# A Hymba-style layer on one core: products 7 and 4 on one-bank accumulators, the late work of two feed-forward tiles spread over 16 steps, four sums moved to GpSimd

## The chip, the core and the metric

The kernel runs on one core of one Trainium2 chip. A core has TensorE (PE in the profile; its weight loads are PEld), VectorE (DVE), ScalarE (ACT), GpSimd (POOL) and SyncE (SP), each with a queue of its own that is worked off in order; they wait for one another through semaphores. SP issues nearly all DMAs. PE writes into PSUM, eight banks of 512 f32 for each of 128 partitions; everything else of the core lives in SBUF. The metric is the device time of one execution in microseconds (us); lower is better.

## The reference

One inference step of a hybrid decoder layer for 1040 prompt tokens (16 meta tokens and 1024 others) and 8 sample tokens, 1048 tokens in all, with width 1024 and a feed-forward width of 2816:

```
h = h + 0.5 * swiglu(rmsnorm(h, n1), w1g, w1u, w1d)      # feed-forward 1
u = rmsnorm(h, nm) @ w_in                                # HGRN2 heads and Mamba-2 heads
h = h + concat(hgrn_out, ssm_out) @ w_out
h = h + 0.5 * swiglu(rmsnorm(h, n2), w2g, w2u, w2d)      # feed-forward 2
def swiglu(x, wg, wu, wd):
    return (jax.nn.silu(x @ wg) * (x @ wu)) @ wd
```

and a final RMSNorm of what remains. All is f32. The change touches the two feed-forward blocks alone: `x @ wg`, `x @ wu`, the product with SiLU, and the preparation of the operands of `@ wd`.

## The kernel before, in words

**Precision.** Every f32 operand is split into a high part and a rest (`hi`: a cast on ACT; `lo`: a subtraction on DVE), and every product is three matmuls: high by high, high by low, low by high (`mm3`, lines 163 to 165). One matmul has 262 columns in the first feed-forward block (Q = 1048/4) and 258 in the second, which works on the 1032 tokens that are left.

**Seven products.** `x @ [wg wu]` is cut into 2 by 2 blocks and computed in Strassen-Winograd form, with products that the code numbers 1 to 7. `Left` (line 468) makes the weights' operands of a 128-column tile of gate and up: `load` brings four pieces (1, 7, 4, 2) by DMA into `r` buffers, `sum_` (line 487, DVE) makes 5, 6, 7 and 3 of them, `hi` (line 491, ACT) and `lo` (line 495, DVE) split each into a `ws` buffer. There are 8 `r` buffers, 6 `ws` buffers and 9 temporaries `t`. The tokens' operands (`Blocks`) are made once and stay.

**Steps.** `Steps` is an order of work written out by hand. `add` appends a step: one product on one half of the tokens (c = 0 or 1), 4 x 3 = 12 matmuls, and what follows it (`post`: the evacuation of PSUM). `before(i, fn)` puts DVE, ACT or SP work ahead of step i; of several things ahead of one step, the one registered first goes first. PE, DVE, ACT and SP execute in the order in which `run` issues, and a queue whose head waits holds all that is behind it. GpSimd is not on that list.

**Units.** Most of a feed-forward block is made of units of two tiles, f = 0 and f = 1 (`two_pairs`, line 860): 9 units in the first block, 10 in the second. Each tile has the six products `ORDER2` = 1, 6, 2, 5, 7, 4, each for both halves: 12 steps. The seventh product, 3, is made for both tiles together with half as many matmuls by a second application of the same algorithm (`Third`): seven small products of 6 matmuls each, which follow steps 3 to 9 of tile f = 1 and use the four one-bank accumulators of the pool `mis` (`psm`). So a unit is 24 x 12 + 7 x 6 = 330 matmuls. Ahead of the units stand one or two single tiles of seven full products (`pair`, line 555), and in the first block also two plain tiles; behind the units stands the down projection (`down`).

**Accumulators.** The pool `acc` has the other four banks, as two buffers of two banks, one bank for each half. Products 1, 6, 5 and 7 begin an accumulator; 2 goes on top of 1, and 4 on top of 7, after the first of each has been read out: what is added is the sum so far.

```
        b = {2: 1, 3: 5, 4: 7}.get(p, p)
            new = p in (1, 6, 5, 7)
```

**What follows the products** (`post`, lines 894 to 908): 1 is copied by ACT (line 896); 6 (line 898), 5 (line 902), 7 (line 904, each half by itself) and 4 (line 907, both halves together) are added by DVE; 2 is multiplied by the norm's factor on DVE (line 885) and goes through SiLU on ACT (line 886). After 4, `out` (lines 889 and 892) scales up and multiplies it with the gate into the unit's hidden tile (`s` buffers, 8 of them). The gate and up parts that need `Third` follow at steps 10 to 13 of tile 1 and a little beyond it (`second`, `out`).

**Operands of the down projection.** `Hidden` takes the four hidden blocks of a unit, makes four differences (`sub`, line 965, DVE) and stores seven blocks to DRAM (`store`, line 968, SP), where `down` reads them later (line 1003). `jobs_apart` places the sums and stores of a unit at steps that mostly lie in the next unit, and earlier in the last unit.

Of the kernel before, what the change touches and what calls it, by code (L numbers as in the profile page):

```python
# [17 lines left out]
P = 128  # L18
# [49 lines left out]
class Core:  # L68
# [21 lines left out]
    def banks(self, n):  # L90

        self.banks_.close()
        self.acc = self.banks_.enter_context(self.tc.tile_pool(name="acc", bufs=4 // n, space=PSUM))
        self.pairs = n == 2

# [374 lines left out]
class Left:  # L470
# [30 lines left out]
    def plan(self, S, s0, late, sums, order=ORDER, loads=(-11, -11, -10, -10)):  # L501
        for ps, ds, fn in (
            ((7, 4, 1, 2) if len(order) == 6 else (1, 7, 4, 2), loads, self.load),
            ((5, 6, 7, 3), [d + sums for d in (-7, -7, -6, -5)], self.sum_),
            (order, [2 * i - 4 + late for i in range(7)], self.hi),
            (order, [2 * i - 3 + late for i in range(7)], self.lo),
        ):
            for p, d in zip(ps, ds):
                S.before(s0 + d, lambda p=p, fn=fn: fn(p))
# [9 lines left out]
class Unit:  # L519


    def __init__(self, K, w, ops, n, post, apart=()):
        self.K, self.w, self.ops, self.n, self.post, self.apart = K, w, ops, n, post, apart
        self.ps = {}
# [12 lines left out]
    def step(self, S, p, c, cs, mis=False):  # L537
# [5 lines left out]
        if p in self.apart:  # L543
            S.add(mm, lambda: self.post(p, slice(c, c + 1), self.bank(p, cs, mis)[:, c : c + 1]))
        else:
            S.add(mm, (lambda: self.post(p, slice(cs[0], cs[-1] + 1), self.bank(p, cs, mis))) if c == cs[-1] else None)
# [164 lines left out]
ORDER2 = (1, 6, 2, 5, 7, 4)  # L711
# [64 lines left out]
class Third:  # L776
# [7 lines left out]
    def plan(self, S, s1):  # L784
        for d, fn, *args in (
            (-2, self.sums, 0),
            (-1, self.sums, 1),
            (0, self.hi, 0),
            (1, self.lo, 0),
            (1, self.hi, 1),  # L790
            (2, self.lo, 1),
            (2, self.sums, 2),
            (3, self.hi, 2),
            (4, self.lo, 2),
            (5, self.hi, 3),
            (6, self.lo, 3),
        ):
            S.before(s1 + d, lambda fn=fn, args=args: fn(*args))
# [61 lines left out]
def two_pairs(K, S, wg, wu, i, ops, spread, hids, sub):  # L860
# [6 lines left out]
    cs = slice(0, 2)  # L867
# [9 lines left out]
    third.plan(S, s1)  # L877
# [6 lines left out]
    def gate(f, n, t, src):  # L884
        nc.vector.tensor_mul(t, src, spread.lanes(n, cs))  # L885
        nc.scalar.activation(t, t, AF.Silu)  # L886

    def out(f, n, u):
        nc.vector.tensor_mul(u, u, spread.lanes(n, cs))  # L889
        if not hids[f]:  # L890
            hids[f].append(K.slot("s", K.T))
        nc.vector.tensor_mul(halves(hids[f][0][:, n * 2 * K.Q : n * 2 * K.Q + 2 * K.Q]), temp(f, f"g{n}"), u)  # L892

    def post(f, p, c, b):
        if p == 1:
            nc.scalar.copy(temp(f, "v"), b)
        elif p == 6:
            nc.vector.tensor_add(temp(f, "v"), b, temp(f, "v"))
        elif p == 2:
            gate(f, 0, temp(f, "g0"), b)  # L900
        elif p == 5:
            nc.vector.tensor_add(temp(f, "g1"), b, temp(f, "v"))  # L902
        elif p == 7:
            nc.vector.tensor_add(temp(f, "u1")[:, c], b, temp(f, "g1")[:, c])  # L904
        elif p == 4:
            u = temp(f, "v")
            nc.vector.tensor_add(u, b, u)
            out(f, 0, u)

    def second(f):  # L910
        g = temp(f, "g1")
        nc.vector.tensor_add(g, g, third.q[f])  # L912
# [1623 lines left out]
```

## Time and profile before

| | us |
|---|---|
| median of three runs | 2018.33 (2015.95 to 2020.79) |
| profiled execution | 2022.06 |
| span of the profiled execution | 2019.8 |
| PE busy in the span | 1937.9 (96%) |
| DVE busy | 1537.6 (76%) |
| ACT busy | 859.2 (43%) |
| POOL busy | 84.7 (4%) |

The span runs from the first instruction to the last; the profiled execution's own time is 2.3 us longer than its span. A line such as L904 is a line of the kernel. `acc<-u,ws` says that an instruction writes the tile `acc` and reads `u` and `ws`, buffer numbers left out. "Idle before, releaser" is the time that an engine stood still ahead of an instruction, and what it had waited for. A matmul of 258 columns is shown with about 285 ns from its start to its end, but matmuls are pipelined, and starts follow one another much closer than that: the time that PE loses is read from the distances of starts, not from the busy time. In the timeline the first column is the start, the second the duration, and the bracket the idle time and its releaser.

The stretches: the units of the first feed-forward block lie at about 122 to 518 us, its down projection after that to about 750 us, the heads up to about 1230 us, the output projection up to about 1300 us, the units of the second block at about 1340 to 1780 us.

### The profile page before, as it was taken

How to read it: one execution, taken by the hardware profiler on the slowest of the kernel's cores; microseconds unless marked ns; L12 is line 12 of the kernel's file. 1: busy time of each engine (PE TensorE's matmuls, PEld its weight loads, DVE VectorE, ACT ScalarE, POOL GpSimd, SP SyncE). 2: the span in 40 equal slices, each digit the busy share in tenths (PEclk: the TensorE clock that was granted, in tenths of full speed). 3: DMA queues.
4: the chain of work that ended last, by engine and by line, in shares of the span. 5: the costliest groups of instructions: out<-in, count | busy, mean ns of one | idle time of the engine just before them, and what ended most of it. 6: DMA issues, size and time to landing. Idle time of an engine off the chain costs nothing.

```text
span 2019.8 us, 41324 instructions
## 1 busy us (share of the span) xinstructions
PE 1937.9 (96%) x16686; PEld 1886.4 (93%) x16686; DVE 1537.6 (76%) x2787; ACT 859.2 (43%) x1642; POOL 84.7 (4%) x144
## 2 busy tenths in 40 slices
PE   9989999999999999999999999989999999999998
PEld 9979999899999999999899989989999989999998
DVE  7878788888789778576575556987778888878974
ACT  6522222323543654466564446632222332353353
POOL 3000000000000320000000002200000000000000
PEclk9999999999999999999999999999999999999999
DMA  7132223223787651231453343222323332488762
GB/s 236 51 114 85 90 85 107 90 82 124 228 262 245 190 179 39 54 105 46 118 167 91 96 148 128 85 84 88 97 84 90 102 93 82 126 228 254 262 188 94
DMA packets 324209, 258.46 MB, mean 128 GB/s; under 512 B 18923, under 2 KB 298731, under 8 KB 324011
## 3 DMA queue, kind: packets, MB, share of 16 engines
q1 hardware_dynamic: 323779, 255.79, 41.3%
q8 instruction: 131, 2.15, 0.4%
q14 instruction: 59, 0.48, 0.1%
q0 software_dynamic: 224, 0.04, 0.0%
q10 hardware_dynamic: 16, 0.00, 0.0%
HBM read 190.79 MB, written 65.05 MB: 127 GB/s over the span
## 4 chain that ended last, share of the span: by engine, by line
PE 74%; DVE 20%; issue 3%; ACT 2%; DMA 1%; POOL 0%; SPq 0%; DVEq 0%; ACTq 0%; POOLq 0%
PE acc L163 21%; PE acc L165 20%; PE acc L164 20%; DVE r L487 3%; DVE ws L495 2%; DVE s L965 2%; DVE s L892 2%; DVE t L885 2%; PE mis L163 2%; PE mis L165 2%; PE mis L164 2%; DVE t L889 1%; DVE t L912 1%; DVE t L904 1%; DVE t L902 1%
## 5 line engine op out<-in xcount | busy, mean ns | idle before, releaser
L163 PE MATMUL acc<-u,ws 128*128 128x258 f32 (+4 forms) x4210 | 1241.4, 295 | 54.4 <-DVE t L904 40.7
L165 PE MATMUL acc<-u,ws 128*128 128x258 f32 (+4 forms) x4210 | 1223.4, 291 | 9.7 <-DVE ws L495 9.7
L164 PE MATMUL acc<-u,ws 128*128 128x258 f32 (+4 forms) x4210 | 1221.2, 290 | 1.1 <-DVE u L376 0.8
L163 PEld LDWEIGHTS acc<-u,ws 128*128 128x128 f32 x4210 | 797.0, 189 | 77.2 <-DVE t L904 32.2
L165 PEld LDWEIGHTS acc<-u,ws 128*128 128x128 f32 x4210 | 797.3, 189 | 15.2 <-DVE ws L495 14.7
L164 PEld LDWEIGHTS acc<-u,ws 128*128 128x128 f32 x4210 | 799.7, 190 | 2.4 <-DVE u L376 1.1
L495 DVE TENSOR_TENSOR ws<-r,ws 128x512 fp32r<-128x512 f32 x264 | 182.4, 692 | 15.7 <-ACT ws L491 15.5
L886 ACT ACTIVATE t<-t 128x516 f32<-128x516 f32 (+1 forms) x76 | 48.6, 640 | 338.0 <-DVE t L885 338.0
L491 ACT CAST ws<-r 128x512 fp32r<-128x512 f32 x264 | 152.9, 616 | 4.8 <-DVE r L487 4.7
L487 DVE TENSOR_TENSOR r<-r,r 128x512 f32<-128x512 f32 x149 | 102.9, 692 | 5.1 <-DMA r<-in_w_ffn_up_dram 3.7
L1011 DVE TENSOR_TENSOR u<-u,u 128x1048 fp32r<-128x1048 f32 (+3 forms) x84 | 97.9, 1166 | 8.6 <-ACT u L1007 8.2
L158 DVE TENSOR_TENSOR ws<-r,ws 128x512 fp32r<-128x512 f32 x88 | 60.9, 701 | 38.7 <-ACT ws L157 38.3
L250 POOL TENSOR_TENSOR t<-t,t 128x262 f32<-128x262 f32 (+1 forms) x56 | 54.5, 985 | 828.3 <-DMA r<-in_w_ffn_down_dram 641.7
L820 ACT CAST ws<-t 128x512 fp32r<-128x512 f32 (+1 forms) x57 | 31.2, 547 | 133.3 <-DVE t L809 85.6
L1069 ACT CAST ws<-u 128x512 fp32r<-128x512 f32 (+1 forms) x72 | 42.2, 585 | 100.4 <-DVE u L1064 92.6
L1007 ACT CAST u<-u 128x1048 fp32r<-128x1048 f32 (+3 forms) x84 | 82.9, 987 | 4.2 <-DMA u<-hd 4.2
L1069 ACT CAST ws<-r 128x512 fp32r<-128x512 f32 (+1 forms) x84 | 48.0, 582 | 71.0 <-DVE r L1064 28.5
L1098 DVE SCALAR_TENSOR_TENSOR s<-acc,s 128x524 f32<-128x524 f32 (+3 forms) x86 | 53.9, 650 | 31.7 <-PE acc L165 31.4
L1074 DVE TENSOR_TENSOR ws<-r,ws 128x512 fp32r<-128x512 f32 (+1 forms) x84 | 57.0, 687 | 25.0 <-ACT ws L1069 24.9
L163 PE MATMUL mis<-u,ws 128*128 128x258 f32 (+1 forms) x228 | 65.0, 285 | 2.2 <-DVE t L852 2.0
L904 DVE TENSOR_TENSOR t<-acc,t 128x258 f32<-128x258 f32 (+1 forms) x76 | 32.6, 428 | 43.8 <-PE acc L165 41.9
L1074 DVE TENSOR_TENSOR ws<-u,ws 128x512 fp32r<-128x512 f32 (+1 forms) x72 | 47.4, 659 | 23.7 <-ACT ws L1069 23.7
(459 smaller groups left out, 2416.8 us busy)
## 6 DMA issues: line engine op xcount, KB each, us to landing
r<-in_w_ffn_down_dram SPq DMA_DIRECT2D x128, 256.0 KB
hd<-s SPq DMA_DIRECT2D x93, 258.0 KB
r<-in_w_ffn_gate_dram SPq DMA_DIRECT2D x88, 256.0 KB
r<-in_w_ffn_up_dram SPq DMA_DIRECT2D x88, 256.0 KB
hd<-s SPq DMA_DIRECT2D x77, 262.0 KB
u<-hd SPq DMA_DIRECT2D x36, 516.0 KB
u<-hd SPq DMA_DIRECT2D x28, 524.0 KB
r<-in_w_in_dram SPq DMA_DIRECT2D x56, 256.0 KB
```

What stands on the lines that cost most here:

```text
L158: self.nc.vector.tensor_sub(lo, src, hi.bitcast(F32))
L163: mm(ps, whi, xhi, start=first, stop=False, skip_group_check=more)
L164: mm(ps, whi, xlo, start=False, stop=False, skip_group_check=more)
L165: mm(ps, wlo, xhi, start=False, stop=last, skip_group_check=more)
L250: K.nc.gpsimd.tensor_add(self.sq[q], self.sq[q], t)
L487: self.K.nc.vector.tensor_tensor(self.raw[p], self.raw[x], self.raw[y], op)
L491: self.K.nc.scalar.copy(self.w[p][:, : self.n * P], self.raw[p])
L495: self.K.nc.vector.tensor_sub(t[:, 512 : 512 + w], self.raw[p], t[:, :w].bitcast(F32))
L1007: K.nc.scalar.copy(hi, lo.bitcast(F32))
L1011: K.nc.vector.tensor_sub(lo, lo.bitcast(F32), hi.bitcast(F32))
L1069: nc.scalar.copy(w[p, j, g][:, : n * P], src)
L1074: nc.vector.tensor_sub(t[:, 512 : 512 + n * P], box[0], t[:, : n * P].bitcast(F32))
```

## The change

- **Accumulators.** The pool `acc` gets two fixed buffers of two banks each, `acc0` and `acc1`. In the units, products 1 and 2 use `acc0`, and 6 and then 5 use `acc1`. Everywhere else (`pair`, `down`) the two are taken in strict turn. Products 7 and 4 of the units go to the one-bank accumulators of `mis`, a bank for each half, beside the four that `Third` takes.
- **Order of the products.** A tile's order is 1, then product 4 of the tile before, then 6, 2, 5, 7. Product 4 of the last tile of a unit comes in the next unit, and of the last unit just ahead of `down`. With d counted from a unit's beginning: 0 and 1 are product 1 of f = 0; 2, 3 product 4 of the tile before; 4, 5 product 6; 6, 7 product 2; 8, 9 product 5; 10, 11 product 7; 12, 13 product 1 of f = 1; 14, 15 product 4 of f = 0; 16 to 23 products 6, 2, 5, 7 of f = 1. `Third`'s seven products follow the steps 14 to 20. The first unit has no product 4 ahead of it and is two steps shorter.
- **Read-out of 4.** DVE adds each half of product 4 by itself.
- **Late work.** What was in `second` and `out` stands at d = 16 to 31. A unit's last 8 of these positions lie in the next unit.
- **Weights.** `plan_apart` loads pieces 7, 4, 1, 2 at 10, 9, 9, 7 steps ahead of a tile, sums 5, 6, 7, 3 at 5, 4, 3, 2 ahead, and splits each operand about four steps ahead of its product.
- **Down's operands.** The four differences of a unit run on GpSimd instead of DVE, and stores and differences have new positions, the same in the last unit. One load of the first product of `down` is a step later.

```diff
-        self.acc = ...tile_pool(name="acc", bufs=4 // n, space=PSUM))
+        self.acc = ...tile_pool(name="acc", bufs=4 if n == 1 else 1, space=PSUM))
+        self.turn = 0
...
-    def psum2(self):
+    def psum2(self, i=None):
         assert self.pairs
-        return self.acc.tile([P, 2, 512], F32, tag="acc", name=self.uid("acc"))
+        if i is None:
+            i, self.turn = self.turn, 1 - self.turn
+        else:
+            self.turn = 1 - i
+        return self.acc.tile([P, 2, 512], F32, tag=f"acc{i}", name=self.uid("acc"))
...
+    def plan_apart(self, S, s0):
+        for fn, at in (
+            (self.load, ((7, -10), (4, -9), (1, -9), (2, -7))),
+            (self.sum_, ((5, -5), (6, -4), (7, -3), (3, -2))),
+            (self.hi, ((1, -4), (6, 0), (2, 2), (5, 4), (7, 6), (4, 10))),
+            (self.lo, ((1, -3), (6, 1), (2, 3), (5, 5), (7, 7), (4, 11))),
+        ):
+            for p, d in at:
+                S.before(s0 + d, lambda p=p, fn=fn: fn(p))
...
 class Third:
-    def plan(self, S, s1):
...
+    def plan(self, S, s0):
+        for fn, at in (
+            (self.sums, (10, 11, 14)),
+            (self.hi, (11, 12, 14, 16)),
+            (self.lo, (12, 13, 15, 17)),
+        ):
...
-def two_pairs(K, S, wg, wu, i, ops, spread, hids, sub):
+def two_pairs(K, S, wg, wu, i, ops, spread, hids, sub, before):
-    s0 = len(S.steps)
-    s1 = s0 + 2 * len(ORDER2)
+    s0 = len(S.steps) - (0 if before else 2)
...
-        lefts[n].plan(S, (s0, s1)[n], 0, 0, ORDER2, (-11, -10, -10, -9))
+        lefts[n].plan_apart(S, s0 + 12 * n)
...
+    def bank(f, p, c):
+        d = banks[f]
+        if p in (7, 4):
+            if c not in d:
+                d[c] = K.psm()[:, : K.Q]
+            return d[c]
+        n = {1: "a", 2: "a", 6: "b", 5: "c"}[p]
+        if n not in d:
+            d[n] = K.psum2(0 if n == "a" else 1)[:, :, : K.Q]
+        return d[n] if c is None else d[n][:, c]
...
         elif p == 4:
-            u = temp(f, "v")
-            nc.vector.tensor_add(u, b, u)
-            out(f, 0, u)
+            nc.vector.tensor_add(temp(f, "v")[:, c], bank(f, p, c), temp(f, "v")[:, c])
...
     for f in range(2):
+        steps(f, 1)
+        if f == 0 and before:
+            before()
+        elif f == 1:
+            steps(0, 4)
+        for p in (6, 2, 5, 7):
+            steps(f, p)
...
+    for d, fn, *args in (
+        (16, lambda: times_r(0, temp(0, "v"))),
+        (16, out, 0, 0),
+        (22, g1, 0),
+        (23, lambda: (times_r(1, temp(0, "g1")), silu(temp(0, "g1")))),
+        (24, lambda: times_r(1, temp(0, "u1"))),
+        (25, out, 0, 1),
+        (26, g1, 1),
+        (28, lambda: (times_r(1, temp(1, "g1")), silu(temp(1, "g1")))),
+        (28, lambda: times_r(0, temp(1, "v"))),
+        (29, out, 1, 0),
+        (30, lambda: times_r(1, temp(1, "u1"))),
+        (31, out, 1, 1),
+    ):
+        S.before(s0 + d, lambda fn=fn, args=args: fn(*args))
+    return s0, lambda: steps(1, 4)
...
-    def parts(self, i, hid):
+    def parts(self, i, hid, apart=False):
+        engine = K.nc.gpsimd if apart else K.nc.vector
...
-            K.nc.vector.tensor_sub(b[p], val(x), val(y))
+            engine.tensor_sub(b[p], val(x), val(y))
...
-    def jobs_apart(self, S, i, hid, s1):
...
+    def jobs_apart(self, S, i, hid, s0):
+        sub, store = self.parts(i, hid, True)
+        for d, args in zip((26, 32, 33, 34), ((5, 12, 1), (6, 3, 5), (7, 3, 12), (4, 2, 6))):
+            S.before(s0 + d, lambda args=args: sub(*args))
+        for d, p in zip((17, 29, 32, 33, 35, 36, 38), (1, 5, 3, 2, 6, 7, 4)):
+            S.before(s0 + d, lambda p=p: store(p))
```

More of the change, by code (lines that the diff above doesn't have):

```diff
@@ L915, in third_step @@
-    def third_step(m):
-        third.mm(m)
-        third.post(m)
-    for f in range(2):
-        unit = Unit(K, lefts[f].w, [o.op for o in ops], 4, lambda p, c, b, f=f: post(f, p, c, b), (7,))
-        for p in ORDER2:
-            for c in range(2):
-                j = len(S.steps) - s1
-                unit.step(S, p, c, (0, 1))
-                if 3 <= j < 10:
-                    S.also(lambda m=SUB[j - 3]: third_step(m))
-    S.before(s1 + 10, lambda: second(0))
-    S.before(s1 + 11, lambda: out(0, 1, temp(0, "u1")))
@@ L929, in two_pairs, with steps, mm @@
-    S.before(s1 + 12, lambda: second(1))
-    S.before(s1 + 13, lambda: out(1, 1, temp(1, "u1")))
-    return s1
+            nc.vector.tensor_add(temp(f, "v")[:, c], bank(f, p, c), temp(f, "v")[:, c])
+    def steps(f, p):
+        for c in range(2):
+            def mm(c=c):
+                new = p in (1, 6, 5, 7)
+                product(K, bank(f, p, c), lefts[f].w[p], ops[c].op[p], 4, new, True, not new)
+            S.add(mm, (lambda c=c: post(f, p, c)) if c == 1 or p in (7, 4) else None)
+            j = len(S.steps) - 1 - s0 - 14
+            if 0 <= j < len(SUB):
+                S.also(lambda j=j: (third.mm(SUB[j]), third.post(SUB[j])))
```

85 lines of the change are left out of this document (31 added, 54 removed).

## The prediction

> **What bounds the kernel now.** First the page's busy shares and the chain that ended last, then PE's waits.
>
> ```profile
> PE 1937.9 (96%) x16686; PEld 1886.4 (93%) x16686; DVE 1537.6 (76%) x2787; ACT 859.2 (43%) x1642; POOL 84.7 (4%) x144
> PEclk9999999999999999999999999999999999999999
> PE 74%; DVE 20%; issue 3%; ACT 2%; DMA 1%; POOL 0%; SPq 0%; DVEq 0%; ACTq 0%; POOLq 0%
> PE acc L163 <- DVE t L904: 40.7, 40, 3.4
> PE acc L165 <- DVE ws L495: 9.7, 23, 0.5
> ```
>
> PE runs at full clock and is the bound; a gain has to be time in which PE stands still. Its largest wait by far is for L904, the read-out of product 7: 40 times, about once for each of the 38 tiles. One unit of the first block in PE's timeline:
>
> ```profile
> 347.26 0.28 PE L165 MATMUL acc<-u,ws 128*128 128x262 f32 x1
> 347.68 0.39 PE L163 MATMUL acc<-u,ws 128*128 128x262 f32 x1
> 347.91 0.28 PE L164 MATMUL acc<-u,ws 128*128 128x262 f32 x1
> 348.65 0.39 PE L165 MATMUL acc<-u,ws 128*128 128x262 f32 x1 [0.46 <-DVE ws L495]
> 349.97 0.28 PE L163 MATMUL acc<-u,ws 128*128 128x262 f32 x1
> 355.69 0.28 PE L165 MATMUL acc<-u,ws 128*128 128x262 f32 x1
> 357.30 0.39 PE L163 MATMUL acc<-u,ws 128*128 128x262 f32 x1 [1.33 <-DVE t L904]
> 358.74 0.28 PE L165 MATMUL acc<-u,ws 128*128 128x262 f32 x1
> 359.64 0.36 PE L163 MATMUL acc<-u,ws 128*128 128x262 f32 x1 [0.61 <-DVE t L904]
> ```
>
> The 48 matmuls from 349.97 to 355.69 follow each other by 5.72/47 = 0.122 us; a step of 12 is 1.46 us. Counted in steps, the row at 347.68 is product 2's first half, 354.35 product 7's first half, 357.30 its second, 359.64 product 4. So the second half of 7 waits for the read-out of the *first* half, in another bank of the same tile, and 4 waits for that of the second. Lost beyond 0.12 a matmul: 0.30 + 0.11 + 0.62 = 1.03 us at product 2, and 1.49 + 0.78 = 2.27 us at 7 and 4; with the slow starts just after each jump (0.1 each) about 1.1 and 2.5: 3.6 us a unit. What DVE and ACT did:
>
> ```profile
> 345.98 0.64 ACT L886 ACTIVATE t<-t 128x524 f32<-128x524 f32 x1 [4.32 <-DVE t L885]
> 347.04 0.59 ACT L896 COPY t<-acc 128x524 f32<-128x524 f32 x1
> 356.01 0.70 DVE L902 TENSOR_TENSOR t<-acc,t 128x524 f32<-128x524 f32 x1
> 356.81 0.43 DVE L904 TENSOR_TENSOR t<-acc,t 128x262 f32<-128x262 f32 x1
> 359.06 0.43 DVE L904 TENSOR_TENSOR t<-acc,t 128x262 f32<-128x262 f32 x1 [1.22 <-PE acc L165]
> 347.68:391.61 43.93, 41.40 (x331) 40.51 (x331) 35.56 (x62) 12.60 (x25) 0.00 (x0) 1.00 0.30 92
> 1403.17:1446.64 43.47, 40.89 (x330) 40.03 (x330) 35.27 (x62) 12.52 (x24) 0.00 (x0) 1.00 0.30 92
> ```
>
> Product 1's copy (L896) waited behind the previous unit's last SiLU, which waited for DVE: the late work bunched at a unit's end. DVE reads 7's first half at 356.81 though the product had ended at about 355.7, being behind with L902. The last two rows are whole units of the two blocks: 43.93 and 43.47 us, against 330 x 0.122 = 40.2 of matmuls. DVE has 35.6 of them.
>
> **The change part by part.** *Stalls in the steady units.* With 7 and 4 a bank for each half, 7's second half waits for nothing; between 7 and 4 of a half lie one 7, two of product 1: three steps, 4.4 us, for a read-out that comes 1.5 to 2.5 us after its product in the rows above. Product 2 now has 4 and 6, four steps, behind product 1's copy (before: 6, two), and the last SiLU ahead of that copy is issued two steps before it. Product 5, in `acc1`, needs 6 read out, with product 2's two steps (2.9 us) between; 1 of the next tile needs 2 read out, four steps earlier. `mis` hands out eight banks a unit from four buffers: 7, 7, four of `Third`, 7, 7. The closest reuse is `Third`'s third bank at d = 17, when the bank of product 4's first half was read out at d = 14, or of the copy at d = 16, one step earlier: covered. The buffers `ws`, `r` and `t` have at most 7, 8 and 8 wanted at once against 6, 8 and 9; the seventh `ws` is `Third`'s last split at d = 16, held until `Third`'s second product has ended; it is wanted at d = 19, three steps on, and DVE's `lo` at d = 17 waits with it, ahead of 6's read-out, which is due a step later. As before, this hides in ACT and DVE time. So all 3.6 us a unit can go: 8 units of the first block with this pattern and 9 of the second, 17 x 3.6 = 61.2 us.
>
> *GpSimd.* Rows of POOL's only large use, and of DVE beside it:
>
> ```profile
> L965 DVE TENSOR_TENSOR s<-s,s 128x524 f32<-128x524 f32 x33 | 22.9, 697 | 0.0
> 389.79 0.70 DVE L965 TENSOR_TENSOR s<-s 128x524 f32<-128x524 f32 x1
> 390.41 0.70 DVE L889 TENSOR_TENSOR t<-t,u 128x524 f32<-128x524 f32 x1
> L2146 POOL TENSOR_TENSOR u<-u,u x3: 1273/1298/1298, 2003.3 to 2005.8; 128x512 f32<-128x512 f32 x2, 8x512 f32<-8x512 f32 x1
> 669.29 6.87 POOL L250 TENSOR_TENSOR t<-t,t 128x262 f32<-128x262 f32 x4 [6.83 <-ACT t L249]
> 673.75 1.80 DVE L1011 TENSOR_TENSOR u<-u,u 128x1048 fp32r<-128x1048 f32 x1
> 675.48 1.24 DVE L1074 TENSOR_TENSOR ws<-r,ws 128x512 fp32r<-128x512 f32 x1
> 677.25 1.24 DVE L1011 TENSOR_TENSOR u<-u,u 128x1048 fp32r<-128x1048 f32 x1
> ```
>
> Four L965 leave DVE, 0.62 us each from start to start (389.79 to 390.41): 2.5 us a unit. On POOL one takes about 1.33 (1298 ns x 524/512). It isn't free to DVE: beside POOL's 262-wide additions the same L1011 takes 1.80 instead of 1.24, and a 512-wide L1074 1.24, where the 524-wide rows above have 0.70: 0.55 us each. Estimated by width, a 524-wide one costs DVE at most 1.1 us; nothing where DVE reads PSUM or waits. Splitting 4's read-out adds 2 x (2 x 0.43 - 0.70) = 0.3. DVE's unit: 35.6 - 2.5 + 0.3 = 33.4, plus 0 to 4.4, so 33.4 to 37.8 against 40.2 of PE. It fits as a sum; the place to look at is d = 5 to 11. There DVE has, at 0.61 a full SBUF operation, 0.7 from PSUM and 0.4 a half: d=5 two and 6's read-out 1.9; d=6 0.6; d=7 three and 2's read-out 2.5; d=8 0.6; d=9 two and 5's 1.9; d=10 1.7; d=11 1.35: 10.6 us in 7 x 1.46 = 10.2, and three of the four GpSimd sums fall into it: up to 3.3 us late at its end. What is due then: product 1's weights at d = 12 (`lo` at d = 9), 4's at d = 14 (`lo` at d = 11), `Third`'s first at the end of d = 14. Counting through in that worst case, they come 0.2 to 0.3 us ahead of PE; from d = 14 a step with its `Third` product is 2.2 us and DVE catches up. So the residue runs from 0 to some 1.5 us a unit; I take 0.4, nearer to zero because the sum above is already the worst overlap: 17 x 0.4 = 7 back.
>
> The Trainium skill, "SBUF — State Buffer", section "SBUF: two separate sides", says that VectorE and GpSimd share a port pair that is locked for a whole instruction, also against a VectorE operation with two SBUF inputs, and that the other blocks fully. The rows agree in kind, with 0.55 us where POOL's own row is longer. Held for the whole 1.33 us it would be 5.3 us a unit and a DVE of 38.7; by that rule the residue would rise by about 0.6 a unit, and the sum end some 10 us higher.
>
> *Queues.*
>
> ```profile
> 125.51 0.56 SPq L481 DMA_DIRECT2D r<-in_w_ffn_up_dram  x1
> 131.80 0.69 DVE L487 TENSOR_TENSOR r<-r,r 128x512 f32<-128x512 f32 x1 [3.71 <-DMA r<-in_w_ffn_up_dram]
> ```
>
> SP issues per unit the same 8 loads and 7 stores. A store waits for its sum and holds the loads behind it. The closest: store 4 at d = 38 (14 of the next unit) stands ahead of loads 7, 4, 1 at 14 and 15. The last sum would end at about d = 34.5 if POOL starts after `out` at d = 31 and runs three times 1.33: two steps early or more. Loads have four steps to the first `sum_`, at least 5.9 us; in the worst case seen (the rows above, 125.51 to 131.80) it took 6.3. Cost 0 to 0.5 a unit, in the 0.4.
>
> *First units, ends and single tiles.*
>
> ```profile
> PE acc L163 <- DVE t L904: 2.5, 2, 1.9
> PE acc L163 <- DVE t L885: 2.0, 1, 2.0
> PE acc L163 <- DVE t L904: 4.0, 2, 3.4
> PE acc L163 <- DVE t L885: 1.2, 1, 1.2
> PE acc L163 <- DVE t L898: 0.8, 1, 0.8
> PE mis L163 <- DVE t L852: 1.0, 1, 1.0
> PE acc L163 <- DVE t L904: 0.4, 1, 0.4
> 1327.42 0.70 DVE L577 TENSOR_TENSOR t<-acc,u 128x516 f32<-128x516 f32 x1 [0.30 <-PE acc L165]
> 80.83 0.70 DVE L577 TENSOR_TENSOR t<-acc,u 128x524 f32<-128x524 f32 x1 [0.34 <-PE acc L165]
> ```
>
> PE's waits in 122 to 143 us (rows 1, 2), 1340 to 1365 (rows 3 to 5) and, the same at 500 to 520 and at 1765 to 1780, rows 6 and 7. First units: 4.5 and 6.0 us; there 5 follows the read-out of 2 (L885), and no longer will. DVE is behind by the `sub` blocks' making; I keep 0.5 and 2.5 of them: 7.5 saved (between 4 and 10.5). Last units: 1.4 each; product 4 now stands directly behind 7, while `down` already claims DVE: I put 2 each, +1 in all (-3 to +5). Single tiles (`pair`): the fixed turn puts product 5 into 2's buffer, so PE stands from 2's end until its read-out: 0.3 + 0.7 = 1.0 us by the last two rows. Three tiles; the middle one already runs behind DVE. +2 (0 to 4). The later load of `down` has five steps still: 0.
>
> Sum: -61 + 7 - 7.5 + 1 + 2 = -58.5, rounded to -60 for the start spacings left out above. The profiled execution, 2022.1, would be 1962; it lies 3.7 above the median, so against 2018.33: **1958 us**. Bounds: all residues at their best -72, 1946; a residue of 1.5 a unit and the worst ends, +19 + 6, 1983.
>
> **The rivals.** (a) *DVE too late in each unit.* POOL's port time lands wholly in d = 7 to 11 and each unit stalls 1.5 us at product 1 or 4, with L495 as releaser: (1.5 - 0.4) x 19 = +21, 1979. For it: 94% of DVE at the upper bound. Against: the sum still fits.
> (b) *Only the wait on L904 goes*; product 2's 1.1 us stays since the copy or the weights still come late: 1958 + 17 x 1.1 = 1977. Against: product 2 has four steps after the copy now, and its `lo` three.
> (c) *The read-outs stay coupled* (it doesn't do what it says): a bank of `mis` comes to 7 only when `Third` leaves it, or the wait was DVE's lag alone; half of the 2.3 stays: 17 x 1.15 = +20 on top of (a), 1999.
> (d) *Slower: GpSimd's hold makes DVE the bound.* Place: POOL's four sums against L487, L495, L889. Decides when DVE's unit passes 43.9: 43.9 - 33.4 = 10.5 us, 2.6 for each sum. POOL's four rows from 669.29 took 6.87 for 262 wide, 1.7 each; doubled, and all of it charged to DVE, that is 3.4 each, a unit of 47.0, +3.1 x 19 = +59: 2077. Against: DVE's rows beside them grew by 0.55 only, a fifth of what it needs.
>
> **How the numbers follow.** The forecast with its own range, 1945 to 1968: 0.60. (a) 0.15, (b) 0.08, (c) 0.04, (d) 0.08; below 1945 0.02; within 0.2% 0.03. What a measurement can tell from no change is about 0.2%, 4 us. Faster: 0.60 + 0.15 + 0.08 + 0.04 + 0.02 = 0.89; slower 0.08. For eight in ten the range has the forecast, (a) and (b): 1944 to 1985.
>
> **What would show it.** Unit periods of 40.2 to 40.8 us instead of 43.9; no wait of PE for L904's successor; product 2 without a jump; DVE at 33 to 38 us a unit, with two-SBUF-input operations lengthened to over a microsecond beside POOL; in `pair` a wait of about 1 us for L577. Wrong would be shown by PE waiting for L495's successor in every unit, by SP standing long at stores, or by new waits at the beginning of `down`.

## The result

| | before | after |
|---|---|---|
| median, us | 2019.01 (2015.95 to 2022.64, six runs) | 1947.08 (1946.03 to 1948.19, six runs) |
| profiled execution, us | 2022.06 | 1947.16 |
| its span, us | 2019.8 | 1945.4 |

The ratio is 0.9643 (0.963 to 0.9655): 71.9 us less, against 60 forecast. The time lies inside the range, near its lower end.

Line numbers of the kernel after: `mm3` is L169 to L171 (before L163 to L165), the copy of product 1 L914, the read-outs of 6, 5, 7 and 4 are L916, L921, L923 and L925, the norm's factor L902, SiLU L905, `out` L910, `sum_` L493 (before L487), `hi` L497, `lo` L501 (before L495), the adding of `Third`'s part L949, `sub` L1001 (before L965), and `pair`'s factor L590 (before L577).

The page of the kernel after, busy shares and the chain that ended last:

```profile
PE 1913.5 (98%) x16686; PEld 1877.1 (96%) x16686; DVE 1542.4 (79%) x2749; ACT 859.7 (44%) x1642; POOL 214.6 (11%) x220
PE 91%; DVE 5%; DMA 1%; ACT 1%; issue 1%; SPq 0%; POOL 0%; DVEq 0%; ACTq 0%; POOLq 0%
```

PE has 91% of the chain where it had 74%, DVE 5% where it had 20%. PE's waits in the kernel after (what it waited for, us in total, times, the longest):

```profile
PE acc L169 <- DVE t L590: 7.1, 3, 5.4
PE mis L169 <- DVE t L923: 3.4, 5, 1.1
PE acc L171 <- DVE ws L501: 2.2, 5, 1.0
```

The read-out of product 7 was waited for 40 times, 40.7 us; five waits, 3.4 us in all, are left, and the 23 waits for `lo` have become five. What is largest now, 7.1 us, lies in the single tiles. Whole units, two of the first block and one of the second, each from the start of its first GpSimd sum to that of the next unit's (columns: length, then busy time and instructions of PE, PEld, DVE, ACT and POOL, granted clock, DMA share, GB/s):

```profile
160.58:200.71 40.13, 40.13 (x333) 40.13 (x332) 35.94 (x60) 12.69 (x24) 6.64 (x4) 1.00 0.34 101
200.71:240.77 40.06, 40.06 (x332) 40.06 (x331) 35.84 (x60) 12.69 (x24) 6.65 (x4) 1.00 0.33 100
1387.18:1426.78 39.60, 39.60 (x333) 39.55 (x332) 35.65 (x60) 12.64 (x24) 6.66 (x4) 1.00 0.34 101
```

The x333 counts every matmul that reaches into the window; 330 start in it. PE is busy in all of a unit, and no two starts of PE are over 0.131 us apart from 160 to 479 us: no stall is left to remove there. A unit takes 40.13 and 39.60 us where it took 43.93 and 43.47.

Both traces have 16686 matmuls on PE, so the start of the n-th in one can be set against the start of the n-th in the other. How far the kernel after is ahead, by stretches:

| stretch and its end (us in the trace of before) | ahead by, us | gained in the stretch |
|---|---|---|
| first matmul of the single tiles, 65.4 | 1.89 | 1.89 |
| end of single and plain tiles, 122.1 | -0.36 | -2.25 |
| first unit of block 1, 170.0 | 5.15 | 5.51 |
| the stalls of eight steady units, 505.0 | 35.17 | 30.02 |
| last unit, 519.0 | 34.71 | -0.46 |
| down, heads, output projection, 1299.2 | 35.04 | 0.33 |
| single tile of block 2, 1338.0 | 34.26 | -0.78 |
| first unit of block 2, 1370.0 | 39.48 | 5.22 |
| the stalls of nine steady units, 1760.0 | 74.63 | 35.15 |
| last unit and the beginning of down, 1790.1 | 74.24 | -0.39 |

### The profile page after: what moved, and what is told of

It reads as the page before. It is cut to its first block, busy times and chain, and to the rows that moved or that the text cites. A ratio compares the mean times of both kernels' runs of the same rounds, so it can differ in the third digit from the quotient of the medians.

```text
span 1945.4 us, 41390 instructions
## 1 busy us (share of the span) xinstructions
PE 1913.5 (98%) x16686; PEld 1877.1 (96%) x16686; DVE 1542.4 (79%) x2749; ACT 859.7 (44%) x1642; POOL 214.6 (11%) x220
## 4 chain that ended last, share of the span: by engine, by line
PE 91%; DVE 5%; DMA 1%; ACT 1%; issue 1%; SPq 0%; POOL 0%; DVEq 0%; ACTq 0%; POOLq 0%
PE acc L169 23%; PE acc L171 22%; PE acc L170 22%; PE mis L169 5%; PE mis L171 5%; PE mis L170 5%; PE mis L1966 1%; DVE ws L501 1%; DMA u<-hd 1%; PE mis L1679 0%; PE mis L2028 0%; PE mis L1673 0%; DMA s<-in_x_prompt_dram 0%; DVE u L382 0%; DVE t L327 0%
## 5 line engine op out<-in xcount | busy, mean ns | idle before, releaser
L169 PE MATMUL acc<-u,ws 128*128 128x258 f32 (+4 forms) x3602 | 1059.2, 294 | 10.3 <-DVE t L590 7.1
L171 PE MATMUL acc<-u,ws 128*128 128x258 f32 (+4 forms) x3602 | 1047.4, 291 | 2.2 <-DVE ws L501 2.2
L170 PE MATMUL acc<-u,ws 128*128 128x258 f32 (+4 forms) x3602 | 1047.5, 291 | 0.2 <-DVE u L330 0.2
L169 PEld LDWEIGHTS acc<-u,ws 128*128 128x128 f32 x3602 | 681.7, 189 | 20.1 <-issue 14.0
L171 PEld LDWEIGHTS acc<-u,ws 128*128 128x128 f32 x3602 | 681.1, 189 | 3.9 <-DVE ws L501 3.5
L170 PEld LDWEIGHTS acc<-u,ws 128*128 128x128 f32 x3602 | 683.4, 190 | 1.3 <-DVE u L330 0.7
L169 PE MATMUL mis<-u,ws 128*128 128x258 f32 (+1 forms) x836 | 237.5, 284 | 3.6 <-DVE t L923 3.4
L171 PE MATMUL mis<-u,ws 128*128 128x258 f32 (+1 forms) x836 | 237.0, 284 | 0.1
L170 PE MATMUL mis<-u,ws 128*128 128x258 f32 (+1 forms) x760 | 214.7, 282 | 0.0
L905 ACT ACTIVATE t<-t 128x516 f32<-128x516 f32 (+1 forms) x76 | 48.6, 640 | 338.1 <-DVE t L902 338.1
L501 DVE TENSOR_TENSOR ws<-r,ws 128x512 fp32r<-128x512 f32 x264 | 181.6, 689 | 3.0 <-ACT ws L497 2.9
L497 ACT CAST ws<-r 128x512 fp32r<-128x512 f32 x264 | 156.2, 614 | 36.0 <-PE mis L171 18.2
L169 PEld LDWEIGHTS mis<-u,ws 128*128 128x128 f32 x836 | 157.8, 189 | 4.7 <-DVE t L923 2.6
L171 PEld LDWEIGHTS mis<-u,ws 128*128 128x128 f32 x836 | 157.6, 189 | 1.1 <-DVE ws L501 0.7
L493 DVE TENSOR_TENSOR r<-r,r 128x512 f32<-128x512 f32 x149 | 147.0, 997 | 0.1
L170 PEld LDWEIGHTS mis<-u,ws 128*128 128x128 f32 x760 | 144.1, 190 | 0.0
L1001 POOL TENSOR_TENSOR s<-s,s 128x516 f32<-128x516 f32 (+1 forms) x57 | 95.2, 1699 | 124.3 <-DVE s L910 124.3
L1001 POOL TENSOR_TENSOR s<-s 128x516 f32<-128x516 f32 (+1 forms) x19 | 32.7, 1723 | 669.0 <-DVE s L910 558.4
```

Of the source, the lines that this page charges most:

```text
L169: mm(ps, whi, xhi, start=first, stop=False, skip_group_check=more)
L170: mm(ps, whi, xlo, start=False, stop=False, skip_group_check=more)
L171: mm(ps, wlo, xhi, start=False, stop=last, skip_group_check=more)
L493: self.K.nc.vector.tensor_tensor(self.raw[p], self.raw[x], self.raw[y], op)
L497: self.K.nc.scalar.copy(self.w[p][:, : self.n * P], self.raw[p])
L501: self.K.nc.vector.tensor_sub(t[:, 512 : 512 + w], self.raw[p], t[:, :w].bitcast(F32))
```

## Experiments

The theory ahead of them: the 2.5 us at products 7 and 4 are a wait for the tile, not for the bank, and go with the one-bank tiles alone; the 1.1 us at product 2 go since its copy and weights have more steps; the sums on GpSimd are worth nothing. The rivals: that the new order is what decouples 7 and 4, that DVE's relief by GpSimd does it, and that it is the spreading of the late work. Ratios below are to the kernel before, run on the same chip.

**One-bank tiles in the kernel before** (`e2_banks_alone`). Order, late work and sums stay as before.

```diff
+    def one(self, c):
+        if c not in self.ps:
+            self.ps[c] = self.K.psm()[:, None, : self.K.Q]
+        return self.ps[c]
...
-            b = self.bank(p, cs, mis)
+            b = self.one(c)[:, 0] if self.apart and p in (7, 4) else self.bank(p, cs, mis)[:, cs.index(c)]
...
-            nc.vector.tensor_add(u, b, u)
-            out(f, 0, u)
+            nc.vector.tensor_add(u[:, c], b, u[:, c])
+            if c.start == 1:
+                out(f, 0, u)
```

> The kernel before, with one part of the change alone: products 7 and 4 of the units on one-bank tiles, each half of 4 read out by itself; order, late work and sums as before. Theory A (7's second half and 4 waited because the two halves share a tile): the two jumps at 7 and 4 (1.49 and 0.78 us) go, product 2's 1.1 us stays, units of 41.6 us and 41.1 us, 19 x 2.3 = 44 us less than before, about 1975. Rival C (VectorE's lag alone was the wait, and the next tile's product 1 between 7 and 4 is what removes it): at least half of the 2.3 us stays at product 4, time 1995 to 2010.

1975.49 us (1974.49 to 1977.47), ratio 0.9771 (0.9757 to 0.9786), as theory A had it. Its largest waits of PE:

```profile
PE acc L165 <- DVE ws L495: 9.4, 22, 0.5
PE acc L163 <- ACT t L901: 5.7, 17, 0.3
PE mis L163 <- DVE t L909: 5.2, 2, 3.5
```

And one unit of it, with the columns above:

```profile
347.00:388.50 41.50, 40.71 (x331) 40.17 (x330) 35.59 (x64) 12.60 (x24) 0.00 (x0) 1.00 0.31 97
```

The unit falls from 43.93 to 41.50, by 2.43, and the wait for 7's read-out (here L909) is gone from the steady units although 4 still stands directly behind 7; the two that are left lie in the two first units, at 134.54 and 1334.01 us. What stays is product 2: its copy (here L901) and its `lo`. So the tile was the wait. This edit alone brings 0.0229 of the ratio, some 46 us of the 72.

**The sums back on DVE** (`e1_sums_dve`).

```diff
-        sub, store = self.parts(i, hid, True)
+        sub, store = self.parts(i, hid)
```

> The changed kernel with down's four differences of a unit back on VectorE, all else as changed. Theory A (the gain is PE's stalls alone; GpSimd's sums give VectorE nothing, since they hold up its two-input operations by about 1.1 us each and save it 0.62 each): VectorE's busy time of a unit falls from 35.9 to about 34.4 us, unit periods stay at 40.1 and 39.6 us, and the time stays within 3 us of the changed kernel's 1947. Rival B (the move to GpSimd carries part of the gain): VectorE falls behind again, periods rise by 0.5 us or more, time 1957 or above.

1945.19 us (1944.44 to 1947.21), ratio 0.9621 (0.9607 to 0.9635), which overlaps the interval of the kernel after: no gain from GpSimd that can be told from none, as theory A had it. A unit of it:

```profile
201.80:241.90 40.10, 40.10 (x332) 40.10 (x332) 34.72 (x64) 12.89 (x24) 0.00 (x0) 1.00 0.33 100
```

The group of `sum_` in it (busy time, mean ns of one, idle time before):

```profile
L493 DVE TENSOR_TENSOR r<-r,r 128x512 f32<-128x512 f32 x149 | 102.1, 687 | 0.1
```

DVE has less to do with the four sums (34.72) than without them (35.94). In the kernel after the same group, and GpSimd's, read:

```profile
L493 DVE TENSOR_TENSOR r<-r,r 128x512 f32<-128x512 f32 x149 | 147.0, 997 | 0.1
L1001 POOL TENSOR_TENSOR s<-s,s 128x516 f32<-128x516 f32 (+1 forms) x57 | 95.2, 1699 | 124.3 <-DVE s L910 124.3
```

The mean `sum_` grows from 687 to 997 ns. DVE's timeline of the kernel after in one unit:

```profile
201.01 1.82 DVE L949 TENSOR_TENSOR t<-s,t 128x524 f32<-128x524 f32 x1
209.46 1.81 DVE L493 TENSOR_TENSOR r<-r,r 128x512 f32<-128x512 f32 x1
211.19 0.69 DVE L902 TENSOR_TENSOR t<-acc,u 128x524 f32<-128x524 f32 x1
211.80 2.92 DVE L493 TENSOR_TENSOR r<-r,r 128x512 f32<-128x512 f32 x2
```

GpSimd's, in the same unit:

```profile
200.71 1.56 POOL L1001 TENSOR_TENSOR s<-s 128x524 f32<-128x524 f32 x1 [26.74 <-DVE s L910]
209.09 5.09 POOL L1001 TENSOR_TENSOR s<-s,s 128x524 f32<-128x524 f32 x3 [6.81 <-DVE s L910]
```

DVE operations with two operands in SBUF that fall on a sum take up to 1.8 instead of 0.69 us; L902 at 211.19, which reads PSUM, is not lengthened. The four lengthened ones (the pair in the fourth row is 1.20 and 1.80, singly) take 3.9 more, while four sums less save 4 x 0.62 = 2.5.

**Each sum twice on GpSimd** (`e6_sums_twice`).

```diff
-            engine.tensor_sub(b[p], val(x), val(y))
+            for _ in range(2 if apart else 1):
+                engine.tensor_sub(b[p], val(x), val(y))
```

> The changed kernel, but each of the four GpSimd differences of a unit is computed twice, one after the other into the same place: twice the time for which GpSimd holds up VectorE. It asks how far the changed kernel is from the rival in which that is the bound. Theory A: VectorE's unit goes from 35.9 to about 39.8 us (3.9 more) against 40.1 of matmuls; bunched as it is around products 5 and 7, PE loses 0.5 to 2 us a unit, with the split of weights as releaser: time 1957 to 1985. Rival G: GpSimd then waits for gaps of VectorE instead of holding it up, VectorE's unit stays below 37, and the time stays within 4 us of 1947.

2002.57 us (2000.41 to 2003.34), ratio 0.9916 (0.9902 to 0.9931): 55 us more than the kernel after, beyond the 1957 to 1985 of theory A. PE's largest waits:

```profile
PE acc L171 <- DVE ws L501: 24.3, 22, 1.4
PE mis L169 <- DVE t L923: 22.7, 22, 1.2
```

A unit of it:

```profile
264.27:307.58 43.31, 40.92 (x331) 40.32 (x331) 39.23 (x60) 12.69 (x24) 13.47 (x9) 1.00 0.31 94
```

Four more sums hold DVE for 39.23 - 35.94 = 3.3 us a unit, and the unit grows by 43.31 - 40.13 = 3.2. Nearly all of it reaches PE: DVE's work would still fit as a sum (39.23 of 40.13), but not in its due places. The kernel after has PE fully covered, but not by enough for this.

**Product 4 directly behind 7 again** (`e3_four_behind_seven`): the kernel after with the old order of products; the splits of a tile's operands and one load of `down` are placed to suit.

```diff
-    s0 = len(S.steps) - (0 if before else 2)
+    s0 = len(S.steps)
...
-            (self.hi, ((1, -4), (6, 0), (2, 2), (5, 4), (7, 6), (4, 10))),
-            (self.lo, ((1, -3), (6, 1), (2, 3), (5, 5), (7, 7), (4, 11))),
+            (self.hi, ((1, -4), (6, -2), (2, 0), (5, 2), (7, 4), (4, 6))),
+            (self.lo, ((1, -3), (6, -1), (2, 1), (5, 3), (7, 5), (4, 7))),
...
-        steps(f, 1)
-        if f == 0 and before:
-            before()
-        elif f == 1:
-            steps(0, 4)
-        for p in (6, 2, 5, 7):
+        for p in (1, 6, 2, 5, 7, 4):
             steps(f, p)
```

> The changed kernel with the order of products of before (4 right behind 7 in its tile, nothing between), the weights split at the places that this order had before; one-bank tiles, late work and GpSimd as changed. Theory A (banks and the spread late work carry the gain): 7 and 4 have one step between for the read-out, PE loses 0 to 0.7 us a unit, time 1947 to 1960. Rival C (the interleaving is needed, since GpSimd's sums make VectorE late by up to 3.6 us just there): 1 to 2.5 us a unit at product 4 or 5, time 1966 to 1995.

1981.36 us (1979.86 to 1982.91), ratio 0.9799 (0.9784 to 0.9814): 34 us more than the kernel after, as rival C had it. PE's largest wait:

```profile
PE mis L169 <- DVE t L923: 30.8, 37, 2.4
```

A unit of it, which begins where PE jumps:

```profile
260.10:302.36 42.26, 40.65 (x331) 40.26 (x331) 35.89 (x60) 13.00 (x25) 6.72 (x5) 1.00 0.32 96
```

DVE's timeline around that jump:

```profile
258.43 1.19 DVE L493 TENSOR_TENSOR r<-r,r 128x512 f32<-128x512 f32 x1
259.54 0.42 DVE L923 TENSOR_TENSOR t<-mis,t 128x262 f32<-128x262 f32 x1
259.88 1.45 DVE L493 TENSOR_TENSOR r<-r,r 128x512 f32<-128x512 f32 x1
261.25 0.68 DVE L501 TENSOR_TENSOR ws<-r,ws 128x512 fp32r<-128x512 f32 x1
261.85 0.42 DVE L923 TENSOR_TENSOR t<-mis,t 128x262 f32<-128x262 f32 x1
```

GpSimd's, there:

```profile
255.72 5.06 POOL L996 TENSOR_TENSOR s<-s,s 128x524 f32<-128x524 f32 x3 [7.38 <-DVE s L910]
```

The same 7 to 4 that waited for nothing in `e2_banks_alone` waits in every unit here, since both read-outs (259.54, 261.85) stand behind `sum_` rows that GpSimd's three sums have lengthened. So the order matters too, with the sums where they are.

**The same with the sums on DVE** (`e8_four_behind_seven_dve`): both edits, to see how much of that loss is GpSimd's.

```diff
-        sub, store = self.parts(i, hid, True)
+        sub, store = self.parts(i, hid)
```

> The kernel with product 4 right behind 7, and with down's four differences back on VectorE besides. With them on GpSimd this order lost 2 us a unit, at 7's read-out. Theory H (the loss is GpSimd's hold on VectorE's two-input operations just there, so the interleaving is the price of the GpSimd sums): most of it goes, unit periods of 40.2 to 40.8 us, time 1947 to 1957. Rival I (VectorE is as late there from its own work, the sums included): 1 us a unit or more stays, time 1966 or above.

1960.51 us (1959.78 to 1963.24), ratio 0.97 (0.9686 to 0.9715), between both expectations: over half of the loss goes. PE's largest wait:

```profile
PE mis L169 <- DVE t L923: 9.1, 20, 2.4
```

A unit of it:

```profile
257.73:298.75 41.02, 40.63 (x331) 40.24 (x331) 34.97 (x64) 13.00 (x24) 0.00 (x0) 1.00 0.32 98
```

DVE's timeline just ahead of the jump at its beginning, with the differences of `down` as L996:

```profile
255.44 0.70 DVE L996 TENSOR_TENSOR s<-s,s 128x524 f32<-128x524 f32 x1
256.05 0.69 DVE L493 TENSOR_TENSOR r<-r,r 128x512 f32<-128x512 f32 x1
257.25 0.42 DVE L923 TENSOR_TENSOR t<-mis,t 128x262 f32<-128x262 f32 x1
```

The 0.9 us a unit that stay are DVE's own queue: the read-out at 257.25 still stands behind a difference, a `sum_` and an L501, now at their ordinary length.

The four runs make a square of ratios: with the new order 0.9643 (GpSimd) and 0.9621 (DVE), with the old 0.9799 and 0.97. GpSimd costs 0.0099, 20 us, in the old order and 0.0022, hardly measurable, in the new. The new order is worth 0.0079, 16 us, without GpSimd, and 0.0156, 31 us, with it.

**The late work bunched as before** (`e5_late_bunched`): order and banks of the kernel after.

```diff
-        (23, lambda: (times_r(1, temp(0, "g1")), silu(temp(0, "g1")))),
-        (24, lambda: times_r(1, temp(0, "u1"))),
-        (25, out, 0, 1),
-        (26, g1, 1),
-        (28, lambda: (times_r(1, temp(1, "g1")), silu(temp(1, "g1")))),
+        (22, lambda: (times_r(1, temp(0, "g1")), silu(temp(0, "g1")))),
+        (23, lambda: times_r(1, temp(0, "u1"))),
+        (23, out, 0, 1),
+        (24, g1, 1),
+        (24, lambda: (times_r(1, temp(1, "g1")), silu(temp(1, "g1")))),
+        (25, lambda: times_r(1, temp(1, "u1"))),
+        (25, out, 1, 1),
...
-        (29, out, 1, 0),
-        (30, lambda: times_r(1, temp(1, "u1"))),
-        (31, out, 1, 1),
+        (28, out, 1, 0),
```

> The changed kernel with the late work bunched at a unit's end as before: the gate and up parts that need the third product at d = 22 to 25, the first half of tile 1 at d = 28. Theory A (product 2's jump went because four steps instead of two lie between product 1's copy and product 2, and the spread as such is not needed): VectorE runs up to 3 us later around the border of two units, PE loses 0 to 0.3 us a unit, time 1947 to 1953. Rival F (the spread is what frees ACT's copy and the weights' splits): a jump of 0.5 to 1.1 us a unit returns at product 6 or 2, time 1957 to 1968.

1978.78 us (1977.79 to 1983), ratio 0.9799 (0.9782 to 0.9815): 0.0156 or 31 us lost, beyond both expectations. Three of PE's largest waits:

```profile
PE acc L171 <- DVE ws L501: 9.3, 22, 1.0
PE mis L169 <- DVE t L923: 8.7, 5, 3.0
PE acc L169 <- ACT ws L497: 7.5, 17, 0.5
```

A unit of it, from the jump on:

```profile
248.10:289.60 41.50, 40.69 (x331) 40.26 (x331) 35.55 (x60) 12.80 (x25) 6.29 (x4) 1.00 0.32 97
```

ACT's timeline just ahead of it:

```profile
246.90 0.64 ACT L905 ACTIVATE t<-t 128x524 f32<-128x524 f32 x1 [5.07 <-DVE t L902]
247.44 0.60 ACT L497 CAST ws<-r 128x512 fp32r<-128x512 f32 x1
```

Product 2 doesn't jump here either: four steps of cover are enough for it. But the last SiLU, waiting for DVE's queue until 246.90, now holds up `hi` of product 6 (247.44), and PE stands at 6 in each unit. The cover moved the loss one product on; the spreading removed it. About 23 of the 31 us are these 1.3 to 1.4 us in 17 units. Part of the rest lies in the two last units: there PE stands 3.0 and 2.9 us for L923 (the second row), and its granted clock is 0.5 for 3.41 and 6.83 us around that.

**Bunched, with product 6's splits two steps earlier** (`e10_bunched_early_split`), ahead of that SiLU.

```diff
-            (self.hi, ((1, -4), (6, 0), (2, 2), (5, 4), (7, 6), (4, 10))),
-            (self.lo, ((1, -3), (6, 1), (2, 3), (5, 5), (7, 7), (4, 11))),
+            (self.hi, ((1, -4), (6, -2), (2, 2), (5, 4), (7, 6), (4, 10))),
+            (self.lo, ((1, -3), (6, -1), (2, 3), (5, 5), (7, 7), (4, 11))),
```

> The kernel with the late work bunched, and with product 6's weights split two steps earlier, which puts that cast ahead of the last SiLU on ACT. Bunched alone it lost 1.4 us a unit at product 6, with ACT's cast and VectorE's split of product 6 as releasers. Theory J (the cast stands in ACT's queue behind the SiLU, which waits for VectorE's late work): the jump goes, at most 0.4 us a unit stays, time 1947 to 1957. Rival K (VectorE is late as such, whatever the order on ACT): the jump moves to product 2 or to the split, time 1965 to 1980.

1975.95 us (1974.95 to 1978.99), ratio 0.9772 (0.9756 to 0.9789), an interval that overlaps that of the run before: hardly better, and in the range of rival K. PE's largest wait:

```profile
PE acc L169 <- DVE t L916: 15.0, 18, 0.8
```

A unit of it, from the jump on:

```profile
252.50:293.90 41.40, 40.56 (x331) 40.25 (x331) 35.54 (x60) 12.79 (x24) 6.29 (x5) 1.00 0.32 97
```

DVE's timeline at the jump:

```profile
251.66 0.70 DVE L916 TENSOR_TENSOR t<-acc,t 128x524 f32<-128x524 f32 x1
```

The jump has gone another product on, to 5, which waits at 252.50 for the read-out of 6; rival K had named product 2 or the split. DVE gets to that at 251.66, after both steps of product 2. What is bunched is DVE's own work; in both runs the next product in line paid.

**`pair` on alternating accumulators** (`e4_pair_banks`): product 2 goes back to the buffer that 5 doesn't take.

```diff
-                self.ps[b, cs] = K.psum2()[:, :, :self.K.Q]
+                self.ps[b, cs] = K.psum2(self.x if b in (1, 7) else 1 - self.x)[:, :, :self.K.Q]
...
-        Unit(K, left.w, [o.op for o in ops], 4, post).both(S)
+        unit = Unit(K, left.w, [o.op for o in ops], 4, post)
+        unit.x = f % 2
+        unit.both(S)
```

> The changed kernel, and in the three single tiles with seven products, product 5 goes into the buffer of 6 and product 7 into that of 2 (turned round from tile to tile), instead of the strict turn. Theory A: the three waits for L590 (0.9, 5.4 and 0.9 us) go; the first and the last are saved, the middle tile is behind VectorE in any case and loses its 5 us elsewhere; 2 us less, 1945. Rival D: the middle tile's wait was the turn's alone, and all 7 us go: 1940. Rival E: waits on the read-out of product 6 take their place: no change.

1943.71 us (1942.77 to 1946.43), ratio 0.9615 (0.96 to 0.963), between theory A and rival D. In 60 to 123 us, where the two single tiles of block 1 lie, PE now waits for the read-outs of 6, 7 and 5 (L597, L606 and L604),

```profile
PE acc L169 <- DVE t L597: 1.6, 1, 1.6
PE acc L169 <- DVE t L606: 1.3, 1, 1.3
PE acc L169 <- DVE t L604: 1.2, 1, 1.2
```

in place of one wait of 5.4 us for L590. All waits of that stretch fall only from 7.0 to 6.1 us. What else goes is a stretch at half clock, which in the kernel after comes with the long standstill (columns as above, the granted clock is the 0.50):

```profile
104.69:111.52 6.83, 4.96 (x23) 4.99 (x24) 4.86 (x8) 2.11 (x4) 0.00 (x0) 0.50 0.34 107
```

There the matmuls from 106.56 to 111.50 start 0.22 us apart instead of 0.12, 2.3 us lost. In this run the clock of 60 to 123 us is 1.00, and the stretch of the single and plain tiles is 2.4 us shorter; 1.1 us more go at the single tile of block 2. So the 2 us that theory A expected came, and more, but in block 1 by the clock and not by the waits. What still stands there is DVE running behind with the making of the tokens' operands, as in the kernel before.

**And that making spread over twice the steps** (`e7_pair_banks_spread`): the edit above and

```diff
-                S.before(at + i, lambda fn=fn, args=args: fn(*args))
+                S.before(at + 2 * i, lambda fn=fn, args=args: fn(*args))
```

> The changed kernel with the buffers of the single tiles turned round as in the run on pair banks, and the making of the third product's token operands spread over twice as many steps. Theory A (the middle single tile and the first unit are late because VectorE has that work there): of the 5.4 us at the middle tile and the 3 us in the second block's first unit about half go, 4 to 6 us less than the changed kernel, 1941 to 1943. Rival: VectorE is as full in the steps that follow, the loss only moves: within 2 us of the run on pair banks.

1936.94 us (1936.03 to 1938.99), ratio 0.9595 (0.958 to 0.9609), below the 1941 to 1943 of theory A. In 60 to 123 us its largest waits are

```profile
PE acc L169 <- DVE t L597: 1.0, 1, 1.0
PE acc L171 <- DVE ws L501: 0.8, 2, 0.5
```

The 0.8 and 1.4 us at the first unit of the second block go too: PE's starts there, 1300 to 1325 us, are never over 0.51 us apart. Of the 11.1 us by which this profiled execution is shorter than that of the kernel after, 6.4 lie in the single and plain tiles of block 1 (2.3 of them the half clock), 1.1 in the single tile and 2.6 in the first unit of block 2; the first unit of block 1 takes 0.6 more. Another 2.0 lie ahead of the first single tile, where nothing was changed and executions differ by more than that. Those tiles' and that unit's loss was DVE's lag behind the making of the operands, and the half clock that came with it.

**That version with the sums on DVE** (`e9_pair_spread_dve`): both edits of `e7_pair_banks_spread` and that of `e1_sums_dve`.

> The run with the single tiles' buffers turned round and the third product's token operands spread, and with down's four differences back on VectorE. Theory A (units have no stall with either engine): same as that run, 1935 to 1938. Rival: with the sums on VectorE something small is gained outside the units (the run with them there alone was 2 us below the changed kernel, within its noise): 1931 to 1934.

1936.49 us (1935.98 to 1938.31), ratio 0.958 (0.9566 to 0.9595): the same as with GpSimd, as theory A had it, and ahead of the kernels before and after.

## Why the prediction was right, step by step

The steps were put against the profiled executions: 2022.06 to 1947.16, 74.9 us, where the sum was 58.5, rounded to 60. The direction, the mechanism and the place were right; the gain was sized too small, most of all by one term, the residue.

- *Steady units, -61.* Right. From the table: 30.02 + 35.15 = 65.2 us in 17 units, 3.8 each instead of 3.6: the slow starts outside the jumps, put at 0.3, add up to 0.5. That the wait was for the tile and not the bank is shown by `e2_banks_alone`. One reading was off, without effect on the sum: the 40 waits for L904 are not one for each tile but two in each unit, both at tile f = 0 (357.30 and 359.64 us, then 401.22 and 403.56); tile f = 1, whose steps `Third` stretches, waits only in the two last units.
- *The residue, 0.4 us a unit, +7.* This step failed. It is 0: PE is busy in 40.13 of 40.13 us. The count of steps d = 5 to 11 took DVE to run 3.3 us late and the weights to arrive 0.2 to 0.3 us ahead; by that count PE waited for nothing even in the worst case, so the 0.4 was a margin that no row of it called for. DVE's unit, 35.94 us, came out inside the 33.4 to 37.8; one doubling of the sums away (`e6_sums_twice`) nearly all of DVE's extra time reaches PE.
- *First units, -7.5 of 10.5.* Too small: 5.51 + 5.22 = 10.7 went. What was kept came out: 0.5 and 2.5 put, none and 2.5 found, the latter as PE's waits in 1305 to 1330 us:

```profile
PE acc L171 <- DVE ws L501: 1.4, 2, 1.0
PE acc L169 <- DVE t L916: 0.8, 1, 0.8
PE mis L169 <- DVE t L923: 0.3, 1, 0.3
```

  The 10.5 was too low: summed from the waits alone, without the slow starts behind each and without the half clock that came with the standstill of 3.4 us (granted clock 0.5 for 3.41 us from 1358.67 us of the trace before), about 1.1 us.
- *Last units, +1.* 0.46 + 0.39 = 0.9. Right.
- *Single tiles, +2, by 1.0 us at each of three.* The net is 2.25 + 0.78 = 3.0, near the forecast partly by luck. The waits for L590 at the first and the last tile are 0.9 each, as sized. At the middle tile PE stands 5.4 us for L590, in place of several waits for DVE in the kernel before, as the step said of that tile and as `e4_pair_banks` shows; but the half clock that comes with this standstill costs 2.3 us and has no term in the sum.
- *Not in the sum:* 1.9 us ahead of the single tiles, all in the first 25 us. They are a difference between executions: the first matmul of the single tiles starts at 61.5 to 65.4 us in the twelve traces, and at 62.8 in `e2_banks_alone`, which has nothing changed up to there against the kernel before with 65.4.

Terms as measured: 65.2 + 10.7 - 0.9 - 3.0 + 0.3 + 1.9 = 74.2. Of the 15.7 us by which the sum of 58.5 was short of that, 7 are the residue, 4 the steady stall, 3 the first units and 2 the start, less 1 for the single tiles. The ranges that the terms were given add up to -75 and -31, a little wider than the -72 and -35 behind the bounds 1946 and 1983; the 71.9 us between the medians lie inside either. The median moved 3 us less than the profiled executions, since the profiled one of before lies 3 us above its median, as the prediction had set off.

*GpSimd's price* was bounded at 0 to 4.4 us a unit on DVE, 1.1 a sum; four took 3.9. Rival (d) needed 2.6 a sum and fell. GpSimd's own row, put at 1.33 us, is 1.56 alone and 1.7 each in a run of three (5.09). The rule of the Trainium skill that was weighed there ("SBUF — State Buffer", section "SBUF: two separate sides") agrees in kind again: operations with two SBUF operands are held, and L902 at 211.19, which reads PSUM, takes its 0.69 us within GpSimd's run of sums. Its lock for a whole instruction fits the rows too, which the prediction had doubted: the DVE operation at 201.01 ends at 202.83, 0.56 us after GpSimd's row (202.27), the pair at 211.80 ends at 214.72, 0.54 after the last of GpSimd's three (214.18), and in `e3_four_behind_seven` it is 261.33 against 260.78. What is added is therefore what is left of GpSimd's row when the DVE operation starts, and not an amount that goes by width; that this came near 1.1 for three of the four is partly luck. Either way the forecast of time stays, since PE waits for neither.

*Rivals (a), (b), (c):* none came. No unit waits for L501 as (a) had it, product 2's jump went, and the read-outs are decoupled. But (b) was set aside for a reason that covers half of the matter: four steps do free product 2, and without the spreading product 6 would have taken its place with 1.4 us a unit (`e5_late_bunched`), close to (b)'s time. The prediction gave the spreading no term of its own; beside the rest of the change it is worth 31 us. Likewise "three steps between 7 and 4" were taken as a help to a wait that, with the late work and the weights placed as before, the banks remove by themselves (`e2_banks_alone`); with them placed as in the change they are needed, 16 us without GpSimd's sums and 31 with them.

## What to carry to other kernels

When two halves of one accumulator tile are produced and read out in turn, look whether the wait between them is for the bank or for the tile: a tile for each half brought, alone, two thirds of this gain. A wait on an engine whose queue is bunched moves to the next product when the waiting one gets more cover; spread the queue, and judge it by due places and not by its sum. Before work is moved to GpSimd, set what it holds on DVE beside what it saves there: here 3.9 us against 2.5.

## What the runs showed of the hardware

- A two-operand sum of 524 f32 columns on GpSimd, 1.56 us in its own row when alone, held the DVE operation with two SBUF operands beside it: that ended 0.54 to 0.56 us after GpSimd's row did, and so took 1.82 and 1.81 us instead of 0.69. The 1.1 us added are more than the 0.62 that a sum costs on DVE. A DVE operation that reads PSUM was not lengthened.
- A standstill of PE of over two us was dearer than its length. After the first 30 us of the twelve traces there are 16 of them, of 2.35 to 5.37 us, and with every one the granted clock falls to 0.5 for 3.41 or 6.83 us, from 2 to 4 us after it began. Matmuls of 262 columns then start 0.22 us apart instead of 0.12. The jumps of 0.4 to 1.6 us in the steady units of the kernel before brought none.
- Where PE waits for nothing, 330 matmuls of 262 columns start in 40.15 us and 330 of 258 in 39.60: 121.7 and 120.0 ns each, the 0.122 us that the prediction counted with.
